# Token columns at other offsets in the rows of the operand tiles

## The chip, the cores and the metric

The kernel runs on one core of a Trainium2 chip. The metric is the device time of one execution in microseconds. The median over three runs of the kernel before is 2046.26 us (2046.22 to 2054.05).

## The reference

One layer of a hybrid decoder on 2048 prompt tokens and 64 sample tokens (8 sequences of 8), all in float32. It normalises x, makes one combined input projection, and runs three branches on its columns: windowed attention (A), a gated short convolution (B) and a chunked spatial MLP (C). Each branch is multiplied with a SiLU path and projected back to the model's width, weighted by a sigmoid gate, summed ("merged") and projected once more:

```python
xn = _rmsnorm(x, p["norm_w"])                       # (tokens, 1024)
h = jnp.einsum("btd,de->bte", xn, p["w_in"])        # all branch inputs and gates
a = jnp.einsum("bte,ed->btd", jax.nn.silu(z_a) * y_a, p["w_out_a"])
b = jnp.einsum("bte,ed->btd", jax.nn.silu(z_b) * y_b, p["w_out_b"])
c = jnp.einsum("bte,ed->btd", jax.nn.silu(z_c) * y_c, p["w_out_c"])
m = gates[:, :, 0] * a + gates[:, :, 1] * b + gates[:, :, 2] * c
return x + jnp.einsum("btd,de->bte", m, p["w_o"])
```

Keys, values, convolution rows and the sample's chunk rows are returned too. The change touches neither their values nor those of y.

## The kernel before, in words

The 2112 tokens are worked through in four super-blocks (the list `SBS`). The first three hold 512 prompt tokens each; the last holds 512 prompt tokens and the 64 sample tokens, and is cut into two chunks of 288 columns. Within a super-block the phases follow one another: keys and values (`kv_phase`), queries (`q_phase`), the z path of A with the attention units spread over it, convolution (`conv_phase`), MLP (`chunk_phase`), gates and merge (`gate_phase`), output projection (`out_phase`).

Every float32 operand of a large matmul is kept as two float32r tiles: a high part, cast on ScalarE (L169), and the low rest, subtracted on VectorE (L170). `gemm_t` multiplies such pairs. For each of 8 (or, for the branches, 4) slices of the contraction it issues three matmuls, at L178, L179 and L180: high weights by high data, high weights by low data, low weights by high data. A weight slice of 128 by 128 is the stationary operand, and 512 (in the last super-block 288) token columns are the moving one. Each matmul has its own weight load.

The data tiles lie in SBUF with the channel on the partition, and with one row of TMAX = 576 float32 columns (2304 bytes) for each slice of the contraction. There are four families:

- `xh`, `xl`: the normalised x, 8 rows each, allocated once;
- `mh`, `ml`: the merged branches, 8 rows each, allocated in `gate_phase`;
- `br0h` to `br2l`: the three branches' outputs, 4 rows each;
- the weights `wh`, `wl`, four buffers each, refilled in turn. They are the stationary operand of `gemm_t`. In `natural` and `wide`, which make keys, values, queries and the MLP's v with the tokens on the partition, the roles are exchanged: slices of 128 tokens of `xh` and `xl` are the stationary operand and the weights move.

In the built program each of these tiles begins at a multiple of 256 bytes. Rows are 2304 bytes (9 times 256), so that every row does too. In the first three super-blocks the 512 token columns start at column 0 of the row. In the last, the first chunk starts at column 0 and the second at column 288, 1152 bytes into the row, which is 128 bytes past a multiple of 256. `xr`, `mr` and `brr` are the functions that give `gemm_t` its moving slices; `xsplit` and `first_block` write `xh` and `xl`.

The order on TensorE and on the DMA queue is the order in the source. Small pieces of work (attention units, preparation of the next super-block) are queued with `later` and put between the matmuls by a count of matmul work (`tick`).

Of the kernel before, what the change touches and what calls it, by code (L numbers as in the profile page):

```python
# [11 lines left out]
F32R = mybir.dt.float32r  # L12
# [4 lines left out]
P = 128  # L17
# [9 lines left out]
TMAX = 576  # L27
# [7 lines left out]
AT_QUERIES, AT_SCORES, AT_PROBS, PROBS_EVERY, AT_VALUES = 0.25, 1.75, 3.5, 0.5, 5.25  # L35
AT_SPATIAL, SPATIAL_EVERY, SPATIAL_AFTER = 2.0, 0.3, 0.35
NEG = -1e30


SBS = [  # L40
# [8 lines left out]
def trunk_kernel(ctx: ExitStack, tc: tile.TileContext, A, O):  # L49
# [118 lines left out]
    def split(hi, lo, src):  # L168
        nc.scalar.copy(hi, src)  # L169
        nc.vector.tensor_tensor(lo, src, hi.bitcast(F32), ALU.subtract)  # L170
# [10 lines left out]
            if k % 2:  # L181
                tick((c1 - c0) / 512 * 0.25)

    xr = (lambda k, a, b: xh[:, k, a:b], lambda k, a, b: xl[:, k, a:b])

    def t_tiles(j, chunks):

# [41 lines left out]
    def xsplit(sb, st):  # L229
        t0, _, chunks, _ = SBS[sb]  # L230
        n = chunks[-1][1]

        def load(k):
            st[k] = st["x"][:, k % 4 * TMAX:k % 4 * TMAX + n]
            nc.sync.dma_start(st[k], A["xt"][k, :, t0 * P:t0 * P + n])

        def piece(k):
            if not k:
                for j in range(4):
                    load(j)  # L240
            x = st[k]
            nc.vector.scalar_tensor_tensor(x, x, nw[:, k:k + 1], st["r"], ALU.mult, ALU.mult)
            split(xh[:, k, :n], xl[:, k, :n], x)
            if k < 4:
                load(k + 4)

        return [lambda k=k: piece(k) for k in range(KT)]

    def first_block():

        xin = res.tile([P, 8 * TMAX], F32, tag="mh", name="xin")
        xnat = res.tile([P, 8 * TMAX], F32, tag="ml", name="xnat")
        r = small.tile([P, 8], F32, tag="xr", name="xr")
        rbuf = res.tile([P, 4 * TMAX], F32, tag="za", name="xrbuf")
        view = lambda t, i: t[:, i * D:(i + 1) * D].rearrange("p (k t) -> p k t", k=KT)

        def load(i, natural):
            if natural:
                nc.sync.dma_start(xnat[:, i * D:(i + 1) * D], A["xn"][i * P:(i + 1) * P])
            else:  # L260
                nc.sync.dma_start(view(xin, i), A["xt"][:, :, i * P:(i + 1) * P].rearrange("k p t -> p k t"))

        def piece(i):
            sq, x = xnat[:, i * D:(i + 1) * D], view(xin, i)
            nc.scalar.activation(sq, sq, AF.Square, accum_out=r[:, i:i + 1])
            rstd(r[:, i:i + 1], r[:, i:i + 1], 1, D)
            ps = ps_tp()
            nc.tensor.transpose(ps[:, 0:P], r[:, i:i + 1].broadcast_to([P, P]), ident)
            ts = slice(i * P, (i + 1) * P)
            rb = rbuf[:, ts]  # L270
            nc.scalar.copy(rb, ps[:, 0:P])
            for k in range(KT):
                nc.vector.scalar_tensor_tensor(x[:, k], x[:, k], nw[:, k:k + 1], rb, ALU.mult, ALU.mult)
                split(xh[:, k, ts], xl[:, k, ts], x[:, k])
            if i == 3:
                ahead.update(loads=RAWS, splits=AHEAD)

        return load, piece


    def natural(o, i, rows, units, n=256):

        ts = slice(i * P, i * P + rows)
        for k in range(KT):
            wh, wl = units[k // 4]
            ws = slice((k % 4) * n, (k % 4 + 1) * n)
            nc.tensor.matmul(o, xh[:, k, ts], wh[:, ws], start=k == 0, stop=False)  # L287
            nc.tensor.matmul(o, xh[:, k, ts], wl[:, ws], start=False, stop=False)  # L288
            nc.tensor.matmul(o, xl[:, k, ts], wh[:, ws], start=False, stop=k == KT - 1)  # L289
            if k % 4 == 3:  # L290
                tick(0.25)
        return o
# [10 lines left out]
    def wide(j0, outs):  # L303

        for u in range(4):
            wh, wl = take("wn", j0 + u)
            for i, (o, rows) in enumerate(outs):
                ts = slice(i * P, i * P + rows)
                for kk in range(2):
                    k = 2 * u + kk  # L310
                    ws = slice(kk * 512, (kk + 1) * 512)
                    nc.tensor.matmul(o, xh[:, k, ts], wh[:, ws], start=k == 0, stop=False)  # L312
                    nc.tensor.matmul(o, xh[:, k, ts], wl[:, ws], start=False, stop=False)  # L313
                    nc.tensor.matmul(o, xl[:, k, ts], wh[:, ws], start=False, stop=k == KT - 1)  # L314
                tick(0.25)
                if u == 3:
                    yield i, o, rows
# [201 lines left out]
    def sample_attention(samp, sbuf, za, br):  # L519
# [85 lines left out]
        later(4.0, lambda: probs(1))  # L605
        later(5.0, values)

    def conv_phase(sb, br):
        _, _, chunks, sample = SBS[sb]
        n = chunks[-1][1]  # L610
        for c in range(4):
            cs = tmp("cs", [P, n])
            for ps, c0, c1 in t_tiles(4 + 4 * c, chunks):
                nc.scalar.copy(cs[:, c0:c1], ps)
            cin = tmp("cin", [P, n + 2])
            nc.vector.tensor_copy(cin[:, 0:2], hist[:, c])
            for ps, c0, c1 in t_tiles(5 + 4 * c, chunks):
                nc.vector.tensor_tensor(cin[:, 2 + c0:2 + c1], ps, cs[:, c0:c1], ALU.mult)
            nc.vector.tensor_copy(hist[:, c], cin[:, 512:514])
            t1 = tmp("t1", [P, n])  # L620
            nc.vector.tensor_scalar_mul(t1[:, 0:512], cin[:, 0:512], cw[:, c, 0:1])
            for r in (1, 2):
                nc.vector.scalar_tensor_tensor(
                    t1[:, 0:512], cin[:, r:r + 512], cw[:, c, r:r + 1], t1[:, 0:512], ALU.mult, ALU.add
                )
            if sample:
                sc = small.tile([P, NS, TS + 2], F32, tag="scin", name="scin", bufs=1)
                nc.sync.dma_start(sc[:, :, 0:2], A["state"][:, c])
                nc.vector.tensor_copy(sc[:, :, 2:], cin[:, 514:578].rearrange("p (n t) -> p n t", n=NS))
                t1s = t1[:, 512:576].rearrange("p (n t) -> p n t", n=NS)  # L630
                nc.vector.tensor_scalar_mul(t1s, sc[:, :, 0:TS], cw[:, c, 0:1])
                for r in (1, 2):
                    nc.vector.scalar_tensor_tensor(t1s, sc[:, :, r:r + TS], cw[:, c, r:r + 1], t1s, ALU.mult, ALU.add)
                nc.sync.dma_start(O["sc"][:, c], sc[:, :, TS:])
                nc.sync.dma_start(O["pc"][:, c], hist[:, c])
            for ps, c0, c1 in t_tiles(6 + 4 * c, chunks):
                nc.vector.tensor_tensor(t1[:, c0:c1], ps, t1[:, c0:c1], ALU.mult)
            z = tmp("z", [P, n])
            for ps, c0, c1 in t_tiles(7 + 4 * c, chunks):
                nc.scalar.activation(z[:, c0:c1], ps, AF.Silu)  # L640
            nc.vector.tensor_tensor(t1, t1, z, ALU.mult)
            split(br[1][0][:, c, :n], br[1][1][:, c, :n], t1)

    def chunk_phase(sb, br, samp_args):
# [9 lines left out]
            for ps, c0, c1 in t_tiles(21 + 2 * c, chunks):  # L654
                nc.vector.tensor_tensor(suc[:, c, c0:c1], ps, suc[:, c, c0:c1], ALU.mult)
        flush()
        br2 = [res.tile([P, 4, TMAX], F32R, tag="br2" + x, name="br2" + x) for x in "hl"]
        br.append(br2)
        vbuf = res.tile([P, 4 * 1024], F32R, tag="mh", name="vbuf")
        def mixed(i, rows, t, gg):  # L660
# [55 lines left out]
    def gate_phase(sb, br):  # L716
        chunks = SBS[sb][2]
        n = chunks[-1][1]
        m = None
        for d in range(KT):  # L720
            acc = None
            for b in range(3):
# [6 lines left out]
                if d == 0 and b == 2:  # L729
                    flush()  # L730
                    m = [res.tile([P, KT, TMAX], F32R, tag="m" + x, name="m" + x) for x in "hl"]
                    if sb + 1 < len(SBS):
                        st, xpieces = xrstd(sb + 1)
                        for j, p in enumerate(xpieces):
                            later(2.0 + 4.0 * j, p)
                    if not sb:
                        later(4.0, lambda: keep("sk", "ck"))
                        later(12.0, lambda: keep("sv", "cvr"))
# [80 lines left out]

    for sb in range(len(SBS)):  # L820
        chunks, sample = SBS[sb][2:]
        samp = kv_phase(sb, None if sb else prepare)
        qn, abuf = q_phase(sb, samp)
        flush()
        if not sb:
            spatial_weights()
        za = res.tile([P, 4, TMAX], F32, tag="za", name="za")
        br = [[res.tile([P, 4, TMAX], F32R, tag=f"br{b}{x}", name=f"br{b}{x}") for x in "hl"] for b in range(2)]
        sbuf = attention(sb, qn, abuf, za, br, 0.0, UNIT_EVERY)
        for c in range(4):  # L830
            for ps, c0, c1 in t_tiles(c, chunks):
                nc.scalar.activation(za[:, c, c0:c1], ps, AF.Silu)
        conv_phase(sb, br)
        chunk_phase(sb, br, (samp, sbuf, za, br))
        m = gate_phase(sb, br)
        out_phase(sb, m)
# [124 lines left out]
```

## Time and profile before

| | |
|---|---|
| median of the runs | 2046.26 us |
| the profiled execution | 2048.72 us |
| its span, first to last instruction | 2047.0 us |
| mean granted TensorE clock | 0.995 |
| TensorE matmuls, busy share | 99% (10887 instructions) |
| weight loads | 86% |
| VectorE, ScalarE, GpSimd | 51%, 41%, 4% |

The profile was taken from one execution, so 2047.0 us is the time against which its rows add up; the execution's own time is 1.7 us longer. A matmul's duration in it runs from its start to a modelled end and overlaps the next matmul. The pace of a stream of matmuls is therefore read from the starts in the timeline, not from the durations.

### The profile page before, as it was taken

To read this page: it belongs to the slowest core of one execution; us is meant where nothing else is said; L and a number is where in the kernel's file an instruction comes from. 1 tells how busy PE (TensorE), PEld (TensorE's weight loads), DVE (VectorE), ACT (ScalarE), POOL (GpSimd) and SP (SyncE) were. 2 spreads that over 40 slices of the span, in tenths; PEclk is the share of its full clock that TensorE was granted. 3 is DMA by queue.
4 is the path that set the end of the run, shared out by engine and by line. 5 is a ranking of instruction groups with operands and counts; after the bars stand their busy time and mean duration, and the time that the engine had idled before them with its cause. 6 is when DMAs were issued, how large, how long until landed. Compare 5 with 4: busy or idle time off the path is not lost.

```text
span 2047.0 us, 27359 instructions
## 1 busy us (share of the span) xinstructions
PE 2016.7 (99%) x10887; PEld 1757.1 (86%) x10887; DVE 1050.9 (51%) x1818; ACT 845.8 (41%) x1462; POOL 83.5 (4%) x134
## 2 busy tenths in 40 slices
PE   6999999999999999999999999999999999999999
PEld 5788888888888888888888888888879999999999
DVE  5686263445588353335478535335537842533332
ACT  4675233332476333333267433333247641322320
POOL 2200000000200000000200000000110000000000
PEclk9999999999999999999999999999999998999999
DMA  6222233336222223336322223334522332222233
GB/s 206 82 83 83 84 101 123 114 119 210 84 82 83 88 78 126 111 93 201 119 83 81 84 82 109 118 108 136 173 83 59 64 114 57 65 85 86 78 104 108
DMA packets 85695, 212.25 MB, mean 104 GB/s; under 512 B 18224, under 2 KB 23344, under 8 KB 85552
## 3 DMA queue, kind: packets, MB, share of 16 engines
q1 hardware_dynamic: 85536, 209.53, 33.2%
q8 instruction: 85, 1.39, 0.3%
q10 hardware_dynamic: 32, 0.98, 0.1%
q14 instruction: 42, 0.34, 0.1%
HBM read 201.46 MB, written 10.00 MB: 103 GB/s over the span
## 4 chain that ended last, share of the span: by engine, by line
PE 93%; DVE 3%; ACT 2%; POOL 1%; issue 0%; DMA 0%; SPq 0%; ACTq 0%; DVEq 0%; POOLq 0%
PE ps_mm L179 26%; PE ps_mm L178 26%; PE ps_mm L180 26%; PE ps_tp L488 1%; PE wideS L313 1%; PE wideS L314 1%; PE wideS L312 1%; POOL qr L166 1%; PE ps_mm L312 1%; PE ps_mm L314 1%; PE ps_mm L313 1%; PE sp L464 1%; PE ps_mm L289 1%; PE ps_mm L287 1%; PE ps_mm L288 1%; PE pv L496 1%
## 5 line engine op out<-in xcount | busy, mean ns | idle before, releaser
L178 PE MATMUL ps_mm<-xh,wh 128*128 128x512 f32 (+1 forms) x2080 | 743.3, 357 | 5.0 <-DVE qn L409 4.5
L180 PE MATMUL ps_mm<-xh,wl 128*128 128x512 f32 (+1 forms) x2080 | 734.4, 353 | 0.0
L179 PE MATMUL ps_mm<-xl,wh 128*128 128x512 f32 (+1 forms) x2080 | 734.3, 353 | 0.0
L170 DVE TENSOR_TENSOR wl<-raw,wh 128x1024 fp32r<-128x1024 f32 x376 | 408.0, 1085 | 576.5 <-ACT wh L169 573.8
L169 ACT CAST wh<-raw 128x1024 fp32r<-128x1024 f32 x376 | 353.5, 941 | 772.1 <-PE ps_mm L179 535.4
L178 PEld LDWEIGHTS ps_mm<-xh,wh 128*128 128x128 f32 x2080 | 393.2, 189 | 51.9 <-issue 4.7
L180 PEld LDWEIGHTS ps_mm<-xh,wl 128*128 128x128 f32 x2080 | 392.6, 189 | 49.6
L179 PEld LDWEIGHTS ps_mm<-xl,wh 128*128 128x128 f32 x2080 | 393.4, 189 | 45.7
L179 PE MATMUL ps_mm<-ml,wh 128*128 128x512 f32 (+1 forms) x320 | 112.5, 351 | 0.3 <-DVE ml L170 0.3
L180 PE MATMUL ps_mm<-mh,wl 128*128 128x512 f32 (+1 forms) x320 | 112.4, 351 | 0.0
L178 PE MATMUL ps_mm<-mh,wh 128*128 128x512 f32 (+1 forms) x320 | 112.4, 351 | 0.0
L744 DVE TENSOR_TENSOR t<-ps_mm,t 128x512 f32<-128x512 f32 (+1 forms) x120 | 71.6, 597 | 73.7 <-PE ps_mm L180 73.7
L728 ACT ACTIVATE t<-ps_mm,c_bg 128x512 f32<-128x512 f32 (+1 forms) x120 | 73.0, 609 | 69.5 <-PE ps_mm L180 69.5
L450 ACT ACTIVATE rbuf<-ps_tp,c_qnw 64x256 fp32r<-64x256 f32 x128 | 60.0, 468 | 39.4 <-DVE rbuf L451 33.4
L179 PEld LDWEIGHTS ps_mm<-ml,wh 128*128 128x128 f32 x320 | 60.0, 188 | 8.0 <-DVE ml L170 0.6
L180 PEld LDWEIGHTS ps_mm<-mh,wl 128*128 128x128 f32 x320 | 60.1, 188 | 7.5
L178 PEld LDWEIGHTS ps_mm<-mh,wh 128*128 128x128 f32 x320 | 60.1, 188 | 7.4
L474 ACT ACTIVATE sbuf<-sbuf,nm 128x256 f32<-128x256 f32 (+1 forms) x128 | 62.8, 492 | 7.1 <-DVE nm L471 6.8
L767 DVE TENSOR_TENSOR xt<-ps_mm,xt 128x512 f32<-128x512 f32 (+1 forms) x40 | 23.9, 597 | 75.1 <-PE ps_mm L180 46.2
L179 PE MATMUL ps_mm<-br2l,wh 128*128 128x512 f32 (+1 forms) x160 | 56.5, 353 | 0.4 <-DVE br2l L170 0.2
L180 PE MATMUL ps_mm<-br2h,wl 128*128 128x512 f32 (+1 forms) x160 | 56.3, 352 | 0.0
L179 PE MATMUL ps_mm<-br1l,wh 128*128 128x512 f32 (+1 forms) x160 | 56.2, 352 | 0.0
(212 smaller groups left out, 2703.3 us busy)
## 6 DMA issues: line engine op xcount, KB each, us to landing
raw<-in_wt SPq DMA_DIRECT2D x208, 512.0 KB
raw<-in_wout SPq DMA_DIRECT2D x96, 256.0 KB
raw<-in_wn SPq DMA_DIRECT2D x40, 512.0 KB
raw<-in_wo SPq DMA_DIRECT2D x32, 512.0 KB
xbuf<-in_xn SPq DMA_DIRECT2D x12, 512.0 KB
xt<-in_xt SPq DMA_DIRECT2D x24, 256.0 KB
out_yt<-xt SPq DMA_DIRECT2D x24, 256.0 KB
xbuf<-in_xt SPq DMA_DIRECT2D x16, 256.0 KB
```

Source lines behind the costliest of these rows:

```text
L169: nc.scalar.copy(hi, src)
L170: nc.vector.tensor_tensor(lo, src, hi.bitcast(F32), ALU.subtract)
L178: nc.tensor.matmul(o, wh[:, ws], rh(k, c0, c1), start=k == 0, stop=False)
L179: nc.tensor.matmul(o, wh[:, ws], rl(k, c0, c1), start=False, stop=False)
L180: nc.tensor.matmul(o, wl[:, ws], rh(k, c0, c1), start=False, stop=k == kts - 1)
L312: nc.tensor.matmul(o, xh[:, k, ts], wh[:, ws], start=k == 0, stop=False)
L313: nc.tensor.matmul(o, xh[:, k, ts], wl[:, ws], start=False, stop=False)
L314: nc.tensor.matmul(o, xl[:, k, ts], wh[:, ws], start=False, stop=k == KT - 1)
L450: nc.scalar.activation(hh[half, :, e], src, AF.Copy, scale=qnw2[es])
L474: nc.scalar.activation(s[:, h, k0:], s[:, h, k0:], AF.Exp, bias=nm[:, h:h + 1], accum_out=den[:, h:h + 1])
L728: nc.scalar.activation(t[:, c0:c1], pg[:, : c1 - c0], AF.Sigmoid, bias=bg[:, 8 * b + d:8 * b + d + 1])
L744: nc.vector.tensor_tensor(t[:, c0:c1], pa[:, : c1 - c0], t[:, c0:c1], ALU.mult)
```

## The change

A table gives three offsets, in columns of 4 bytes, for each super-block: for the x tiles, the merged tiles and the branch tiles. The token columns of these tiles are written and read that many columns further right in their rows. The last super-block fills its 576 columns and keeps offset 0.

```diff
+SHIFT = [(4, 1, 20), (12, 6, 8), (2, 32, 14), (0, 0, 0)]
...
-    xr = (lambda k, a, b: xh[:, k, a:b], lambda k, a, b: xl[:, k, a:b])
+    off = [0]
+    xr = tuple(lambda k, a, b, t=t: t[:, k, off[0] + a:off[0] + b] for t in (xh, xl))
...
-            split(xh[:, k, :n], xl[:, k, :n], x)
+            o = SHIFT[sb][0]
+            split(xh[:, k, o:o + n], xl[:, k, o:o + n], x)
...
-                split(xh[:, k, ts], xl[:, k, ts], x[:, k])
+                os = slice(SHIFT[0][0] + i * P, SHIFT[0][0] + (i + 1) * P)
+                split(xh[:, k, os], xl[:, k, os], x[:, k])
...
-        ts = slice(i * P, i * P + rows)
+        ts = slice(off[0] + i * P, off[0] + i * P + rows)
...
+    def branch(sb, name):
+        t = res.tile([P, 4, TMAX], F32R, tag=name, name=name)
+        return t[:, :, SHIFT[sb][2]:SHIFT[sb][2] + SBS[sb][2][-1][1]]
...
-        br2 = [res.tile([P, 4, TMAX], F32R, tag="br2" + x, name="br2" + x) for x in "hl"]
+        br2 = [branch(sb, "br2" + x) for x in "hl"]
...
+                    m = [x[:, :, SHIFT[sb][1]:SHIFT[sb][1] + n] for x in m]
...
     for sb in range(len(SBS)):
         chunks, sample = SBS[sb][2:]
+        off[0] = SHIFT[sb][0]
...
-        br = [[res.tile([P, 4, TMAX], F32R, tag=f"br{b}{x}", name=f"br{b}{x}") for x in "hl"] for b in range(2)]
+        br = [[branch(sb, f"br{b}{x}") for x in "hl"] for b in range(2)]
```

In bytes, the token columns then begin at these places of a row:

| super-block | x | merged | branches |
|---|---|---|---|
| 0 | 16 | 4 | 80 |
| 1 | 48 | 24 | 32 |
| 2 | 8 | 128 | 56 |
| 3 | 0 | 0 | 0 |

The tiles themselves stay where they are, and so do the weights. The instructions of every engine, their order, their sizes and the semaphores that they wait for are the same as before, row for row; only start addresses within the three families differ.

More of the change, by code (lines that the diff above doesn't have):

```diff
@@ L307, in wide @@
             for i, (o, rows) in enumerate(outs):
-                ts = slice(i * P, i * P + rows)
+                ts = slice(off[0] + i * P, off[0] + i * P + rows)
                 for kk in range(2):
```

## The prediction

> **What bounds the kernel now.** I read the page first, then the chain of waits, then the four super-blocks as windows, and last the timeline of TensorE, since its durations overlap.
>
> The page's first part, and the shares of the chain of waits by engine:
>
> ```profile
> PE 2016.7 (99%) x10887; PEld 1757.1 (86%) x10887; DVE 1050.9 (51%) x1818; ACT 845.8 (41%) x1462; POOL 83.5 (4%) x134
> ...
> PE 93%; DVE 3%; ACT 2%; POOL 1%; issue 0%; DMA 0%; SPq 0%; ACTq 0%; DVEq 0%; POOLq 0%
> ```
>
> TensorE is never long without a matmul, and the chain lies on it for 93% of the span. VectorE and ScalarE have half their time free. So the time is the number of matmuls times their pace, and an edit counts if it changes that pace or makes TensorE wait.
>
> The windows of the four super-blocks (us, PE busy with its count, PEld, DVE, ACT, POOL, granted clock, DMA share, GB/s):
>
> ```profile
> 0.00:501.00 501.00, 482.60 (x2226) 400.79 (x2227) 271.09 (x488) 219.88 (x389) 25.79 (x44) 1.00 0.38 120
> 501.00:981.00 480.00, 478.51 (x2239) 398.64 (x2238) 256.05 (x420) 203.03 (x339) 18.40 (x28) 1.00 0.35 108
> 981.00:1462.00 481.00, 479.49 (x2238) 399.38 (x2237) 257.42 (x420) 204.95 (x342) 19.14 (x30) 1.00 0.35 109
> 1462.00:2047.00 585.00, 576.10 (x4189) 558.30 (x4187) 266.38 (x490) 217.93 (x392) 20.13 (x32) 0.99 0.28 82
> ```
>
> The granted clock is full in the first three, the ones that the change touches. Their idle time is 18 us in the first and 1.5 us in each of the next two.
>
> Now the pace itself. The timeline of TensorE in an output projection of super-block 1: two starts of the same line, 24 matmuls apart.
>
> ```profile
> 970.21 0.39 PE L178 MATMUL ps_mm<-mh,wh 128*128 128x512 f32 x1
> ...
> 975.65 0.39 PE L178 MATMUL ps_mm<-mh,wh 128*128 128x512 f32 x1
> ```
>
> 5.44 us for 24 matmuls is **226.7 ns** each. The same in the last super-block, where the second chunk (from 128 bytes past a multiple of 256) runs from 2033.71 to 2036.91, and then a first chunk (from a multiple of 256) to 2040.07, again 24 matmuls each:
>
> ```profile
> 2033.71 0.29 PE L178 MATMUL ps_mm<-mh,wh 128*128 128x288 f32 x1
> ...
> 2036.91 0.29 PE L178 MATMUL ps_mm<-mh,wh 128*128 128x288 f32 x1
> ...
> 2040.07 0.30 PE L178 MATMUL ps_mm<-mh,wh 128*128 128x288 f32 x1
> ```
>
> That is 133.3 ns for the second chunk and 131.7 ns for the first. Same weights, same width, same engine work around them: only the start of the moving operand differs, by 1152 bytes, and **the pace differs by 1.7 ns**. This is the one comparison in this trace of two placements, and it says that placement is not wholly without effect.
>
> From 512 and 288 columns a slope follows: (226.7 - 133.3) / 224 = 0.417 ns for a column. 512 columns are then 213.4 ns, and **13.3 ns** of every matmul are something else (11.7 ns in the first chunk). What it is, the rows show only in part. The stream after four transposes in super-block 0:
>
> ```profile
> 180.28 0.40 PE L179 MATMUL ps_mm<-xl,wh 128*128 128x512 f32 x1
> ...
> 182.13 0.39 PE L178 MATMUL ps_mm<-xh,wh 128*128 128x512 f32 x1
> ```
>
> Eight matmuls in 1.85 us: 231.3 ns each, 4.6 ns slower than the settled stream, with nothing but their history to tell them from it. The weight loads run beside the matmuls and begin with them:
>
> ```profile
> 2036.91 0.29 PE L178 MATMUL ps_mm<-mh,wh 128*128 128x288 f32 x1
> 2036.92 0.19 PEld L179 LDWEIGHTS ps_mm<-ml,wh 128*128 128x128 f32 x1
> ```
>
> So the fixed part depends on how the reading of the moving columns and the next weight load fall against each other in time, and a stream needs some ten matmuls to find its settled place. I read it as two streams that meet at SBUF; that is an interpretation, and the trace names no cause.
>
> **The change part by part.** It adds and removes no instruction, moves none, and changes no size and no wait. What is left are addresses.
>
> *Moving operands.* The matmuls of `gemm_t` in the first three super-blocks all start elsewhere in their rows. Their count is the 512-wide groups:
>
> ```profile
> L178 PE MATMUL ps_mm<-xh,wh 128*128 128x512 f32 x1248 | 493.2, 395 | 0.0
> ...
> L178 PE MATMUL ps_mm<-mh,wh 128*128 128x512 f32 x192 | 74.7, 389 | 0.0
> ...
> L178 PE MATMUL ps_mm<-br1h,wh 128*128 128x512 f32 x96 | 37.4, 390 | 0.0
> ```
>
> Each of these has two like it at L179 and L180, and there are three branches: 3 x (1248 + 192 + 3 x 96) = **5184** matmuls. At 226.7 ns they are 1175 us, so a nanosecond on each is 5.2 us of the whole.
>
> The price per matmul is in no row, since before no 512-wide operand starts off a multiple of 256. Its bounds: downwards the whole fixed part, -13.3 ns, which is -68.9 us; upwards the unsettled stream as a lasting state, +4.6 ns, which is +23.8 us. The nearest row is the pair of chunks, where a placement took 1.7 ns off. I take **-2.5 ns**: a fifth of the fixed part, nearer to that row than to the end, and more than it because eight of the nine new placements are off a multiple of 64 bytes, so that the two streams no longer begin in step. 5184 x 2.5 ns = **-13.0 us**. The sign is the weak point: the same pair of rows can be read as +1.7 ns for the chunk that starts off the multiple.
>
> By the page "TensorE: Matmul & The Clock Gate" of the Trainium skill (Back-to-back issue gap) a warm matmul of 512 columns takes N/2.4 + 2.5 ns, 215.8 ns. Here the trace does not agree: 226.7 ns. If the offsets brought all 5184 to that figure, the estimate by this page would be -56 us, inside the bound above.
>
> *Stationary operands.* In `wide` and `natural` the shifted x tiles are the stationary operand:
>
> ```profile
> L312 PE MATMUL wideS<-wh,xh 128*128 128x512 f32 x128 | 50.5, 394 | 0.0
> ...
> L287 PE MATMUL ps_mm<-wh,xh 128*128 128x256 f32 x128 | 38.9, 304 | 5.7 <-ACT xh L169 5.7
> ```
>
> With the groups into the other PSUM tiles, three quarters of 3 x 256 and of 3 x 128 are in the first three super-blocks, 864 matmuls. Between the same bounds they are worth -11.5 to +4.0 us. The weight load beside them has room (its 0.19 us against 0.227), so I take nothing.
>
> *Writes.* ScalarE and VectorE write the shifted tiles:
>
> ```profile
> L169 ACT CAST mh<-t 128x512 fp32r<-128x512 f32 x24 | 14.9, 621 | 34.2 <-DVE t L748 34.2
> ...
> L170 DVE TENSOR_TENSOR ml<-t,mh 128x512 fp32r<-128x512 f32 x24 | 16.6, 692 | 13.1 <-ACT mh L169 13.1
> ```
>
> If an unaligned write were a tenth slower, that is 0.06 us an instruction, behind engines that are busy half the time. TensorE waits for these tiles almost nowhere but in the first block:
>
> ```profile
> PE ps_mm L287 <- ACT xh L169: 5.7, 5, 4.3
> ...
> PE ps_mm L289 <- DVE xl L170: 0.9, 2, 0.7
> PE ps_mm L179 <- DVE ml L170: 0.3, 1, 0.3
> PE ps_mm L179 <- DVE br2l L170: 0.2, 1, 0.2
> ```
>
> 7.1 us in all; a tenth on it is 0.7 us. I take nothing, and +0.7 us as the upper end. No DMA reads or writes the shifted tiles, so the queues are as before.
>
> *Sum.* -13.0 us on the profiled span of 2047.0 us gives 2034.0 us. The median of the runs stands 0.7 us below that span; the same difference on the median gives 2046.26 - 13.0 = **2033 us**, 0.6% less. A measurement of this kernel can tell about 0.5% from no change.
>
> **Rivals.**
>
> *No effect.* The settled pace is 226.7 ns whatever the offset, because the fixed part is a hand-over inside TensorE that knows no address. For it: the 512-wide rows of x, merged and branch tiles all run at one pace although their rows and the weight buffers lie at many addresses, and the second chunk's 133.3 ns is just the slope plus the same 13.3 ns. Against it: the first chunk's 131.7 ns. It gives 2046 us, with the other terms 2040 to 2050.
> "TensorE: Matmul & The Clock Gate" of the Trainium skill (Step-by-step: what each phase is for) is on this side: it says that TensorE has two independent read ports into SBUF and that loading the next weights takes no bandwidth from the running matmul. If so, two starts could not clash, and the estimate is no change; the 1.7 ns between the chunks and the 4.6 ns of the unsettled stream are what this trace has against it.
>
> *Slower: the streams no longer settle.* With all starts at multiples of 256 bytes the three operands of a step are alike, and the pattern settles after some ten matmuls. With a start off such a multiple each row needs a further piece of memory at its end, and the phase found may be the unsettled one for good. Place: every `gemm_t` of the first three super-blocks. Price: 4.6 ns x 5184 = +23.8 us, 2070 us. It decides from a mean pace of 228.7 ns on (+2.0 ns x 5184 = 10.4 us, 0.5%). For it: the 231.3 ns stretch exists, and so does the second chunk's higher pace. Against it: the unsettled stream passes by itself each time.
>
> *Much faster.* The whole fixed part, or half of it, is a clash that the offsets remove: -6.7 ns to -13.3 ns, -35 to -69 us, 2012 to 1977 us. For it: 13.3 ns is much for a hand-over beside a weight load that has long ended. Against it: no placement in the trace comes near it.
>
> *The change does not do what it says.* Addresses that stay the same would give 2046 us. The slices are plain column offsets on both the writing and the reading side, so I give this 1 in 100, within "no effect".
>
> **How the numbers follow.** Forecast, a few nanoseconds less (2012 to 2041 us): 0.33. Much faster: 0.12. No effect: 0.29. Slower: 0.26. Of the forecast's 0.33 about 0.05 ends within 0.5% (above 2036 us). So faster by over 0.5%: 0.28 + 0.12 = 0.40; within 0.5%: 0.29 + 0.05 = 0.34; slower: 0.26. The range for 8 in 10 leaves about a tenth below, for a removal of more than 8 ns on each matmul (5184 x 8.3 ns = 43 us, 2003 us), and a tenth above for a price over the unsettled stream's: 2003 to 2070 us. As both signs hold much, the likeliest case's own range, 2012 to 2041 us, stands beside it.
>
> **What would show it.** In the changed profile the 24-matmul distances in an output projection of super-blocks 0, 1 and 2 would be about 5.38 us instead of 5.44; 5.44 in all three is the no-effect case, 5.55 the slower one, 5.28 or less much faster. The paces may differ among the three super-blocks and among x, merged and branch tiles, and show which offset does what. The last super-block must stay at 585 us and at 133.3 and 131.7 ns. VectorE's and ScalarE's means for the shifted writes, 692 and 621 ns, should stay; if they grow and TensorE's waits with them, the path was in the writes after all. If the clock in the first three windows falls below 1.00, the cause is none of these.

## The result

The changed kernel takes 2076.35 us (median), against 2047.92 us for the kernel before in the same comparison: a ratio of **1.0131**, 95% interval 1.0103 to 1.0159. It is slower by 1.3%; the forecast was 2033 us, 0.6% faster, and the range ended at 2070 us. Of the four executions of the changed kernel three lie between 2074.96 and 2076.80 us; the fourth took 5313.27 us at full clock, was not profiled, and stands outside the ratio. The profiled execution took 2076.8 us with a span of 2075.1 us, 28.1 us more than before.

The windows of the changed kernel, cut where its super-blocks begin (columns as before):

```profile
0.00:512.00 512.00, 493.56 (x2227) 401.64 (x2228) 271.41 (x488) 220.19 (x389) 25.58 (x44) 0.99 0.38 118
512.00:1002.00 490.00, 489.03 (x2239) 399.72 (x2238) 256.17 (x420) 202.88 (x340) 18.40 (x28) 1.00 0.34 106
1002.00:1492.00 490.00, 488.98 (x2241) 400.11 (x2240) 257.32 (x421) 204.40 (x343) 19.17 (x31) 1.00 0.34 107
1492.00:2075.00 583.00, 574.20 (x4185) 556.39 (x4184) 266.16 (x490) 217.53 (x392) 20.00 (x32) 0.99 0.28 82
```

The counts of matmuls per super-block are those of before to within four. Each of the first three windows is 9 to 11 us longer, and TensorE is busy for all of it: idle time is again 18 us in the first and 1 us in the next two. The last super-block, whose offsets are 0, kept its time. So the loss is pace, and it lies exactly where the offsets are. The granted clock of the first window reads 0.99 instead of 1.00, which the prediction had named as a sign against itself. It comes from the stretch of 10 to 100 us (0.96); the kernel with all offsets at 64 columns, below, has the same 0.96 there and takes the time of the kernel before, and from 100 us to the end of the third super-block the clock is 1.00. So it is not the cause.

The timeline of TensorE in the three output projections, first matmuls of two tiles, 144 matmuls apart:

```profile
472.50 0.40 PE L180 MATMUL ps_mm<-mh,wh 128*128 128x512 f32 x1
...
506.58 0.40 PE L180 MATMUL ps_mm<-mh,wh 128*128 128x512 f32 x1
...
962.70 0.40 PE L180 MATMUL ps_mm<-mh,wh 128*128 128x512 f32 x1
...
996.30 0.39 PE L180 MATMUL ps_mm<-mh,wh 128*128 128x512 f32 x1
...
1452.52 0.39 PE L180 MATMUL ps_mm<-mh,wh 128*128 128x512 f32 x1
...
1486.12 0.39 PE L180 MATMUL ps_mm<-mh,wh 128*128 128x512 f32 x1
```

34.08, 33.60 and 33.60 us: **236.7 ns** a matmul with the merged tile at column 1, **233.3 ns** at column 6, **233.3 ns** at column 32, where it was 226.7 ns in all three.

Where the rest went, from the groups of TensorE by shape: first two of before, then the same and the merged one of the changed kernel (its L181 and L182 are L179 and L180 of before).

```profile
L180 PE MATMUL ps_mm<-xh,wl 128*128 128x512 f32 x1248 | 487.3, 390 | 0.0
L179 PE MATMUL ps_mm<-xl,wh 128*128 128x512 f32 x1248 | 487.2, 390 | 0.0
```

```profile
L180 PE MATMUL ps_mm<-xh,wh 128*128 128x512 f32 x1248 | 499.6, 400 | 0.0
L181 PE MATMUL ps_mm<-xl,wh 128*128 128x512 f32 x1248 | 493.8, 396 | 0.0
L182 PE MATMUL ps_mm<-xh,wl 128*128 128x512 f32 x1248 | 493.3, 395 | 0.0
...
L181 PE MATMUL ps_mm<-ml,wh 128*128 128x512 f32 x192 | 76.1, 396 | 0.0
```

The x groups grew by 6.4, 6.6 and 6.0 us, 19.0 us together; the merged ones by 1.4 us each (74.7 before), 4.2 us. These are sums of modelled durations. Added up from each start to the next, the x matmuls took 19.2 us more, the merged ones 4.5 and the branches 3.8: 27.4 us for the 5184 matmuls, **5.3 ns** each. The wide phases have another 4.4 us, and the remaining matmuls took some 4 us less, which is no more than executions of one kernel differ by. The other engines did not change. The groups of ScalarE and VectorE that write the merged tiles:

```profile
L171 ACT CAST mh<-t 128x512 fp32r<-128x512 f32 x24 | 14.9, 622 | 34.5 <-DVE t L758 34.5
...
L172 DVE TENSOR_TENSOR ml<-t,mh 128x512 fp32r<-128x512 f32 x24 | 16.6, 692 | 13.2 <-ACT mh L171 13.1
```

And the waits of TensorE for the x tiles (us in total, times, longest):

```profile
PE ps_mm L292 <- ACT xh L171: 5.2, 6, 3.5
```

A shifted write takes 622 and 692 ns as before (621 and 692), and TensorE waits 5.2 us for them instead of 5.7.

### The profile page after: what moved, and what is told of

The parts are those of the page before. It is cut to its first block, busy times and chain, and to the rows that moved or that the text cites. A ratio compares the mean times of both kernels' runs of the same rounds, so it can differ in the third digit from the quotient of the medians.

```text
span 2075.1 us, 27359 instructions
## 1 busy us (share of the span) xinstructions
PE 2045.8 (99%) x10887; PEld 1757.8 (85%) x10887; DVE 1051.1 (51%) x1818; ACT 845.0 (41%) x1462; POOL 83.2 (4%) x134
## 4 chain that ended last, share of the span: by engine, by line
PE 92%; DVE 3%; POOL 2%; ACT 1%; issue 1%; DMA 0%; SPq 0%; ACTq 0%; DVEq 0%; POOLq 0%
PE ps_mm L181 26%; PE ps_mm L180 26%; PE ps_mm L182 26%; PE ps_tp L493 1%; PE wideS L318 1%; PE wideS L319 1%; PE wideS L317 1%; POOL qr L168 1%; PE sp L469 1%; PE ps_mm L317 1%; PE ps_mm L319 1%; PE ps_mm L318 1%; PE sp L468 1%; PE pv L500 1%; PE pv L501 1%
## 5 line engine op out<-in xcount | busy, mean ns | idle before, releaser
L180 PE MATMUL ps_mm<-xh,wh 128*128 128x512 f32 (+1 forms) x2080 | 748.8, 360 | 5.0 <-DVE qn L414 4.5
L181 PE MATMUL ps_mm<-xl,wh 128*128 128x512 f32 (+1 forms) x2080 | 740.2, 356 | 0.0
L182 PE MATMUL ps_mm<-xh,wl 128*128 128x512 f32 (+1 forms) x2080 | 739.7, 356 | 0.0
L180 PEld LDWEIGHTS ps_mm<-xh,wh 128*128 128x128 f32 x2080 | 393.3, 189 | 57.1 <-issue 4.7
L182 PEld LDWEIGHTS ps_mm<-xh,wl 128*128 128x128 f32 x2080 | 392.7, 189 | 55.2
L181 PEld LDWEIGHTS ps_mm<-xl,wh 128*128 128x128 f32 x2080 | 393.6, 189 | 50.4
L181 PE MATMUL ps_mm<-ml,wh 128*128 128x512 f32 (+1 forms) x320 | 113.9, 356 | 0.3 <-DVE ml L172 0.3
L182 PE MATMUL ps_mm<-mh,wl 128*128 128x512 f32 (+1 forms) x320 | 113.8, 356 | 0.0
L180 PE MATMUL ps_mm<-mh,wh 128*128 128x512 f32 (+1 forms) x320 | 113.8, 355 | 0.0
L181 PEld LDWEIGHTS ps_mm<-ml,wh 128*128 128x128 f32 x320 | 60.1, 188 | 9.5 <-DVE ml L172 0.6
L180 PEld LDWEIGHTS ps_mm<-mh,wh 128*128 128x128 f32 x320 | 60.1, 188 | 8.9
L182 PEld LDWEIGHTS ps_mm<-mh,wl 128*128 128x128 f32 x320 | 60.1, 188 | 8.9
L181 PE MATMUL ps_mm<-br2l,wh 128*128 128x512 f32 (+1 forms) x160 | 56.9, 356 | 0.2
L182 PE MATMUL ps_mm<-br2h,wl 128*128 128x512 f32 (+1 forms) x160 | 56.7, 355 | 0.0
L182 PE MATMUL ps_mm<-br0h,wl 128*128 128x512 f32 (+1 forms) x160 | 56.7, 354 | 0.0
```

The lines of the kernel that those rows point to most:

```text
L180: nc.tensor.matmul(o, wh[:, ws], rh(k, c0, c1), start=k == 0, stop=False)
L181: nc.tensor.matmul(o, wh[:, ws], rl(k, c0, c1), start=False, stop=False)
L182: nc.tensor.matmul(o, wl[:, ws], rh(k, c0, c1), start=False, stop=k == kts - 1)
```

## The experiments

The question is what "elsewhere" means to TensorE: the absolute start of the moving operand, its place against the weight load beside it, or any start but the first column. Unless something else is said, a pace is the distance of the first and last row shown over the 144 matmuls between them, in an output projection.

### Offsets of 256, 128 and 64 bytes

```diff
-SHIFT = [(4, 1, 20), (12, 6, 8), (2, 32, 14), (0, 0, 0)]
+SHIFT = [(64, 64, 64), (32, 32, 32), (16, 16, 16), (0, 0, 0)]
```

> All three families at column 64 (256 bytes) in super-block 0, 32 (128 bytes) in 1 and 16 (64 bytes) in 2. Theory A (the moving operand's absolute start counts: a read of 512 columns that begins off a multiple of 256 bytes touches one more piece): output projection 226.7 ns a matmul in super-block 0 and 233.3 ns, as the change has it at 128 bytes, in 1 and 2. Theory B (only the position of moving operand and weight load to each other counts, modulo 256 bytes): the same three numbers. Theory C (any other start than the row's first column costs): 231 to 237 ns in all three. Theory D (a piece is 64 bytes): 226.7 ns in all three, which the 233.3 ns at 128 bytes in the change already speaks against.

Timeline of TensorE, super-blocks 0, 1 and 2 in turn:

```profile
461.69 0.39 PE L180 MATMUL ps_mm<-mh,wh 128*128 128x512 f32 x1
...
494.33 0.39 PE L180 MATMUL ps_mm<-mh,wh 128*128 128x512 f32 x1
...
949.62 0.39 PE L180 MATMUL ps_mm<-mh,wh 128*128 128x512 f32 x1
...
983.08 0.40 PE L180 MATMUL ps_mm<-mh,wh 128*128 128x512 f32 x1
...
1434.19 0.39 PE L180 MATMUL ps_mm<-mh,wh 128*128 128x512 f32 x1
...
1467.15 0.39 PE L180 MATMUL ps_mm<-mh,wh 128*128 128x512 f32 x1
```

226.7 ns at 64 columns, 232.4 ns at 32, 228.9 ns at 16. Theories C and D fall: the shift as such is free at 256 bytes, and multiples of 64 bytes are not free. A and B both stand in outline; neither had 228.9 ns.

### Offsets of 4, 16 and 32 bytes

```diff
+SHIFT = [(1, 1, 1), (4, 4, 4), (8, 8, 8), (0, 0, 0)]
```

> All three families at column 1 (4 bytes) in super-block 0, 4 (16 bytes) in 1 and 8 (32 bytes) in 2. If every start off 256 bytes costs the same further piece: 233.3 ns in the output projection of all three. If the odd column costs more by itself, as the merged tile's 236.7 ns at 4 bytes in the change suggests: 236.7 ns in super-block 0, 233.3 ns or less in 1 and 2. If 16 or 32 bytes are a unit of reading: 226.7 ns in 1 or 2. Whole: about 2080 us.

```profile
478.50 0.40 PE L180 MATMUL ps_mm<-mh,wh 128*128 128x512 f32 x1
...
512.58 0.40 PE L180 MATMUL ps_mm<-mh,wh 128*128 128x512 f32 x1
...
966.61 0.40 PE L180 MATMUL ps_mm<-mh,wh 128*128 128x512 f32 x1
...
999.97 0.40 PE L180 MATMUL ps_mm<-mh,wh 128*128 128x512 f32 x1
```

236.7 ns at column 1, as in the change; 231.7 ns at 4; super-block 2, at 8, has 233.3 ns. The span is 2079.8 us. The odd column costs most of the three, and 16 or 32 bytes are no free unit.

### Everything 128 bytes further, weights included

An unused pad tile ahead of the large tiles is made smaller. No column is shifted.

```diff
-    consts.tile([P, 48], F32, name="pad")
+    consts.tile([P, 16], F32, name="pad")
```

> The kernel before, with its unused pad tile 128 bytes smaller, so that all large tiles, weights included, begin 128 bytes past a multiple of 256, and no column is shifted. Theory A (absolute start): every 512-wide matmul at 233.3 ns, the span about 35 us longer. Theory B (position to each other): 226.7 ns, the span as before, 2046 us. The second chunk of the last super-block then starts at a multiple of 256: A has 131.7 ns for it and 133.3 ns for the first, B 133.3 and 131.7 as before.

Super-block 0 in its output projection, and then three chunk starts of the last super-block, 24 matmuls apart: a first chunk to 2030.91, a second to 2034.11.

```profile
463.29 0.39 PE L178 MATMUL ps_mm<-mh,wh 128*128 128x512 f32 x1
...
495.93 0.39 PE L178 MATMUL ps_mm<-mh,wh 128*128 128x512 f32 x1
...
2027.75 0.29 PE L178 MATMUL ps_mm<-mh,wh 128*128 128x288 f32 x1
...
2030.91 0.29 PE L178 MATMUL ps_mm<-mh,wh 128*128 128x288 f32 x1
...
2034.11 0.29 PE L178 MATMUL ps_mm<-mh,wh 128*128 128x288 f32 x1
```

226.7 ns, and a span of 2044.2 us. Every moving operand starts 128 bytes off, where the change had 233.3 ns, and nothing is lost. The chunks keep their paces too, 131.7 and 133.3 ns, although now the second starts at a multiple of 256. **The absolute start (theory A) is refuted**: what counts is where the moving operand lies against something that moved along.

### Only the weights moved

The tile that lies just ahead of the weight buffers is made 8, and in another kernel 16, columns longer, so that the weights begin 32 or 64 bytes later while the three families stay. (The smaller buffers behind the weights move along; none of them is an operand of the matmuls whose paces are read here.) The *place* of a moving operand is from here on its start less that of the weights, in columns, modulo 64, which is 256 bytes.

```diff
-        st["r"] = res.tile([P, TMAX], F32, tag="acc", name="acc")[:, :n]
+        st["r"] = res.tile([P, TMAX + 8], F32, tag="acc", name="acc")[:, :n]
...
+SHIFT = [(0, 0, 0), (32, 32, 32), (48, 48, 48), (0, 0, 0)]
```

> All weight buffers begin 32 bytes later. Columns shifted by 0, 32 and 48 in super-blocks 0, 1 and 2, so that the moving operand stands at -8, +24 and +40 columns against the weights. Theory B: super-block 0 is slow although nothing of x, merged or branches is shifted in it: about 233 ns, as +8 was. The other two between 228 and 234 ns. The last super-block has -8 and +24 in its two chunks, where it had 0 and +32: no forecast of the sign, since 256-wide matmuls with shifted operands ran at 115.6 to 118.3 ns instead of 120.0; between 128 and 136 ns.

Super-block 0, in which no column is shifted:

```profile
474.46 0.40 PE L180 MATMUL ps_mm<-mh,wh 128*128 128x512 f32 x1
...
508.06 0.40 PE L180 MATMUL ps_mm<-mh,wh 128*128 128x512 f32 x1
```

233.3 ns: moving the weights alone costs what moving the data costs. The super-blocks at +24 and +40 columns have 233.3 and 234.3 ns. In the last one, at -8 and +24, the two chunks exchange their paces; a first chunk from 2065.43, a second to 2071.79:

```profile
2065.43 0.30 PE L180 MATMUL ps_mm<-mh,wh 128*128 128x288 f32 x1
...
2068.63 0.30 PE L180 MATMUL ps_mm<-mh,wh 128*128 128x288 f32 x1
...
2071.79 0.30 PE L180 MATMUL ps_mm<-mh,wh 128*128 128x288 f32 x1
```

133.3 ns in the first and 131.7 in the second. So a 288-wide stream at +24 is as fast as one at 0, where a 512-wide one loses 6.7 ns: which places cost something depends on the width.

The kernel with 16 columns, offsets 64, 13 and 16:

> All weight buffers begin 64 bytes later. Columns shifted by 64, 13 and 16: +48, -3 and 0 against the weights. Theory B: 226.7 ns in super-block 2, though both operands start off multiples of 256 bytes there; super-block 0 near the 228.9 ns that +16 had, if the pace is the same for -16; 231 to 237 ns in super-block 1. A theory in which a start off a multiple of 256 bytes costs by itself: 229 to 233 ns in super-block 2. The last super-block has -16 and +16 in its chunks: between 128 and 136 ns.

Super-blocks 1 and 2:

```profile
974.57 0.40 PE L180 MATMUL ps_mm<-mh,wh 128*128 128x512 f32 x1
...
1009.13 0.40 PE L180 MATMUL ps_mm<-mh,wh 128*128 128x512 f32 x1
...
1458.62 0.39 PE L180 MATMUL ps_mm<-mh,wh 128*128 128x512 f32 x1
...
1491.26 0.39 PE L180 MATMUL ps_mm<-mh,wh 128*128 128x512 f32 x1
```

Super-block 2 has operand and weights both 64 bytes off and runs at 226.7 ns: theory B is confirmed from both sides. Super-block 1, three columns before the weights, has 240.0 ns, the slowest found. Super-block 0, at +48, which is -16 modulo 64, has 233.3 ns and not the 228.9 of +16, so the sign matters. The two chunks of the last super-block, at -16 and +16, have 133.3 and 132.2 ns.

### One family undone

```diff
+SHIFT = [(0, 1, 20), (0, 6, 8), (0, 32, 14), (0, 0, 0)]
```

> The change with the x tiles back at column 0, merged and branch tiles shifted as in the change. If each matmul pays for the place of its own operands: 226.7 ns again wherever x is read, 236.7, 233.3 and 233.3 ns in the output projections, some 231 to 233 ns in the branch matmuls. 192 x (10.0 + 6.7 + 6.7) ns + 288 x (4.7 + 6.0 + 4.8) ns = 9.0 us over the kernel before: a span of about 2055 us, and 19 of the 28 us belong to x. If the loss came from writes or from elsewhere: not so divided.

```profile
core 0: 2053.2 us, clock 0.997
```

The kernel before, run beside it on the same chip, has a span of 2042.9 us at the same clock. So 10.3 us of the loss are left, where 9.0 were expected; from start to start the merged and branch matmuls have 8.3 of them. The other two thirds of the change's 28.1 us belong to x, as the group rows say, and the wide phases, where x is the stationary operand, are back at 226.7 ns from 233.3, 233.3 and 230.7 (the median over groups of six, start to start).

### Matched weights at fine offsets

The weights of the branch projections fill half of their buffers, so they can be put as far to the right as the branch tiles.

```diff
+            d = SHIFT[i * len(SBS) // len(units)][2] if n == 512 else 0
-            split(wh[:, :n], wl[:, :n], loaded[i][:, :n])
+            split(wh[:, d:d + n], wl[:, d:d + n], loaded[i][:, :n])
```

First with the change's offsets:

> The change, with the weights of the branch projections (512 columns in buffers of 1024) put as many columns to the right as the branch tiles: 20, 8 and 14. Theory B (the position of moving operand and weight load to each other): the branch matmuls go back to 226.7 ns but for a few after each gate tile, from 231.4, 232.7 and 231.4 ns; the span falls by about 4 us from the change's. If both ends must lie on a line of their own: no better than in the change, or worse, up to 236.7 ns.

This expectation failed. The branch matmuls ran at about 231 to 234 ns, hardly other than in the change, and the span is 2076.9 us. A possible reason is the shifted x matmuls around them, so the next kernel keeps x and merged tiles at column 0:

> x and merged tiles at column 0, the branch tiles at 20, 8 and 14 as in the change, and the weights of the branch projections the same number of columns to the right. The run before this one with matched branch weights had the x tiles shifted too, and its branch matmuls stayed at 230 to 234 ns. If that came from the shifted x stream around them (12 branch matmuls are too few to settle): 226.7 ns here in all three. If a common shift of 80, 32 or 56 bytes is not like one of 64 or 128 (start addresses within a smaller unit count by themselves): above 228 ns in one or more of the three.

and the last one takes 4, 16 and 24 columns for both:

> x and merged tiles at column 0, the branch tiles and the weights of the branch projections both at column 4 (16 bytes) in super-block 0, 16 (64 bytes) in 1, 24 (96 bytes) in 2. In the earlier run with both at 8 columns the branch matmuls came back to 226 and 227 ns after eight matmuls; at 20 and 14 they did not within their twelve. If a common shift must be a multiple of 32 bytes: super-blocks 1 and 2 settle to 226 and 227 ns within the twelve, 0 stays at 230 to 234 ns. If 64 bytes: only 1 settles. If any common shift does and the earlier failures were too short a stream: no such order.

A branch projection has only 12 matmuls between two gate tiles at column 0. Their distances in ns, read from the starts in the two traces, one projection of each offset:

```
 4 columns, 16 bytes   233 228 231 229 232 228 231 228 233 228 231 230
 8 columns, 32 bytes   231 223 231 237 228 232 231 226 227 227 226 235
14 columns, 56 bytes   234 235 233 231 236 233 231 236 233 231 237 236
16 columns, 64 bytes   228 230 232 237 224 230 236 228 233 231 227 226
20 columns, 80 bytes   230 234 230 232 232 230 231 231 231 231 232 232
24 columns, 96 bytes   236 233 235 225 231 236 227 233 230 228 226 227
```

At 8, 16 and 24 columns the stream reaches 226 to 227 ns before its end, at 4, 14 and 20 it does not within twelve. Taking the shift of x away was not enough: over all projections the mean is 231.4 and 233.8 ns at 20 and 14 columns. With a common shift by 32, 64 or 96 bytes the stream can reach its full pace, but it spends seven to ten distances on the way there: the means are 229.5, 230.1 and 231.4 ns at 8, 16 and 24 columns, where the kernel before has 226.8. The kernel with 4, 16 and 24 columns has a span of 2051.7 us, 4.2 us more than the kernel before beside it, so in these short streams matching the weights does not win the loss back. At 4 and 14 columns the distances repeat in turns of two and three from early on, which looks more like a lasting cycle than like a stream on its way. Whether it would last is not shown: no long stream could be given such a shift, because the other weights fill their buffers.

The whole kernel 32 bytes off, by the pad tile:

> The kernel before, with its unused pad tile 32 bytes smaller: all large tiles, weights included, begin 32 bytes before a multiple of 256, and no column is shifted. If only the place of operand and weight load to each other counts, down to 32 bytes: 226.7 ns everywhere and the span of the kernel before, within 4 us. If each must also lie on a multiple of 64 bytes: 231 to 234 ns and a span some 25 to 35 us longer.

```profile
462.27 0.39 PE L178 MATMUL ps_mm<-mh,wh 128*128 128x512 f32 x1
...
494.91 0.39 PE L178 MATMUL ps_mm<-mh,wh 128*128 128x512 f32 x1
```

226.7 ns, span 2045.8 us: 32 bytes in common are free in long streams too.

### Only the high or only the low tiles

The offsets of the high and of the low tiles are taken apart: low at 8 columns in super-block 0, high at 8 in 1, low at 32 in 2.

```diff
+SHIFT = [(0, 8), (8, 0), (0, 32), (0, 0)]
...
-                    m = [x[:, :, SHIFT[sb][1]:SHIFT[sb][1] + n] for x in m]
+                    m = [x[:, :, c:c + n] for x, c in zip(m, SHIFT[sb])]
```

> Only the low tiles (every third matmul's moving operand) at column 8 in super-block 0, only the high ones (two of three) at 8 in 1, only the low ones at 32 in 2. If each pair of a running matmul and the load beside it pays by itself: 226.7 + 6.7/3 = 228.9 ns in 0 and 2, 231.1 ns in 1. If one operand out of step keeps the whole stream from settling: 231 to 234 ns in all three.

```profile
473.32 0.40 PE L181 MATMUL ps_mm<-mh,wh 128*128 128x512 f32 x1
...
506.92 0.40 PE L181 MATMUL ps_mm<-mh,wh 128*128 128x512 f32 x1
...
960.52 0.39 PE L181 MATMUL ps_mm<-mh,wh 128*128 128x512 f32 x1
...
993.80 0.39 PE L181 MATMUL ps_mm<-mh,wh 128*128 128x512 f32 x1
```

233.3 ns with one operand in three out of place, as much as with all three; 231.1 ns with two in three, and 231.1 ns in super-block 2. The 231.1 ns of super-block 1 would also fit a toll on each shifted operand; the other two, where 228.9 ns was expected by it, do not. Nor do the single distances of super-block 0: they repeat 233, 236 and 231 ns, so all three matmuls are slow, and not only one in three. One operand out of place slows the whole stream. That fits a settled state that is lost, not a toll for each matmul.

### A shorter weight load

The output projection uses 64 weight columns in super-block 1 and 32 in 2, in the kernel before. It leaves the other output rows there without their projection:

```diff
-        o = ps[:, : c1 - c0]
+        o = ps[:mc, : c1 - c0]
...
-            ws = slice(k * P, (k + 1) * P)
+            ws = slice(k * P, k * P + mc)
```

> The kernel before, with the output projection using 64 of the 128 weight columns in super-block 1 and 32 in 2, and so computing half and a quarter of its output rows there (the rest keeps the residual x alone); super-blocks 0 and 3 as before. If the fixed 13.3 ns of a matmul come from the weight load's reads getting in the way of the moving operand's: about 6.7 ns and 3.3 ns are left, 220 ns in super-block 1 and 217 in 2. If they are a hand-over that knows nothing of the load's size: 226.7 ns in all.

```profile
944.69 0.40 PE L178 MATMUL ps_mm<-mh,wh 128*64 128x512 f32 x1
...
977.81 0.40 PE L178 MATMUL ps_mm<-mh,wh 128*64 128x512 f32 x1
...
1424.98 0.39 PE L178 MATMUL ps_mm<-mh,wh 128*32 128x512 f32 x1
...
1458.34 0.39 PE L178 MATMUL ps_mm<-mh,wh 128*32 128x512 f32 x1
```

230.0 and 231.7 ns: a smaller load, which also gives fewer output rows, is slower. Both theories fall, the hand-over that knows nothing of the load's size and the load that gets in the way by its length. With 96 columns, and with the merged tile at column 8 for the short loads:

> The output projection uses 96 weight columns in super-block 0, 64 in 1 and 32 in 2 (and computes only so many of each 128 output rows there), with the merged tiles at column 8 in 1 and 2 and nothing else shifted. With the merged tiles at column 0, 64 and 32 weight columns gave 230.0 and 231.7 ns. If the pace falls by 3.3 ns for each 64 further weight columns: 228.3 ns in super-block 0. If the place matters through the load's own reading, less of it leaves less to disturb, and all settle near one pace: 231 to 234 ns in 1 and 2, the shift adding less than the 6.7 ns that it adds at 128 columns. If the shift adds by itself: 236.7 and 238.3 ns.

```profile
463.86 0.39 PE L180 MATMUL ps_mm<-mh,wh 128*96 128x512 f32 x1
...
496.98 0.39 PE L180 MATMUL ps_mm<-mh,wh 128*96 128x512 f32 x1
...
944.20 0.39 PE L180 MATMUL ps_mm<-mh,wh 128*64 128x512 f32 x1
...
977.44 0.39 PE L180 MATMUL ps_mm<-mh,wh 128*64 128x512 f32 x1
```

230.0 ns at 96 columns, 230.8 ns at 64 with the shift (230.0 without), and 233.3 ns at 32 with the shift (231.7 without). Where the load is short the shift adds 0.8 and 1.7 ns, not 6.7. So 226.7 ns is a state that a 512-wide stream reaches with full loads in step with it; take away either, and it runs at 228.9 ns or more in these runs.

### The same mechanism at a harmless offset

```diff
+SHIFT = [(64, 64, 64), (64, 64, 64), (64, 64, 64), (0, 0, 0)]
```

> All three families at column 64 in super-blocks 0 to 2: the whole mechanism of the change, at an offset that keeps operands and weights at the same place modulo 256 bytes. If the loss is that place alone: 226.7 ns everywhere, a ratio to the kernel before within 0.3% of 1. If shifted writes or a start off the row's first column cost anything: longer, up to the change's 1.3%.

The ratio to the kernel before is 0.9999, interval 0.9989 to 1.0009. The slices, the shifted writes and starts that are not the row's first column cost nothing. The loss of the change is the choice of its numbers.

All paces of a 512-wide output projection with full loads, by the place of the moving operand against the weights, in columns modulo 64:

| columns | 0 | 1 | 4 | 6 | 8 | 16 | 24 | 32 | 40 | 48 | 56 | 61 |
|---|---|---|---|---|---|---|---|---|---|---|---|---|
| ns | 226.7 | 236.7 | 231.7 | 233.3 | 233.3 | 228.9 | 233.3 | 232.4 to 233.3 | 234.3 | 233.3 | 233.3 | 240.0 |

None of the eleven other places is as fast as 0, where the kernel before has its 512-wide operands.

## Why the prediction was wrong

**The bound** was read rightly. The time is the number of matmuls times their pace; no wait, write, queue or clock took part. The mean granted clock was 0.995 in both executions.

**The step that failed is the price per moving operand**, -2.5 ns, and in it the sign: the changed kernel shows +5.3 ns on average. I had two rows for it: 131.7 and 133.3 ns in the two chunks, and 231.3 ns after the transposes. I read the chunks as "a placement took 1.7 ns off", and argued that a start off 64 bytes would keep the two streams from beginning in step, and that this would help. The runs show the contrary for 512 columns: in step, at place 0, is the fast state. The first chunk is the one at place 0 and the second the one at 32, in whatever absolute place (shown by moving everything by 128 bytes). Read so, the pair of rows said +1.7 ns for leaving place 0. The prediction named this reading as its weak point and then took the other. But that reading too would have had the sign right by luck: when the weights alone moved, the 288-wide chunk at +24 was as fast as the one at 0. A pair of 288-wide rows could give neither size nor sign for 512 columns.

**The rival "the streams no longer settle"** is what happened. Its place is confirmed, every large matmul of the first three super-blocks; its cause nearly: a 512-wide stream at place 0 passes through 231 ns to 226.7 within ten matmuls, and elsewhere it stays at 229 to 240 ns over a whole output projection. Its price was set too low. 4.6 ns was taken as the upper bound because it was the slowest stretch in the trace, but a passing state is no bound on lasting ones: the merged tiles pay 10.0, 6.7 and 6.7 ns. The range ended at that bound, 2070 us, and so missed 2076 us. Its own reason, a further piece of memory at the end of each row, is refuted: rows that begin 128 bytes off run at full pace if the weights do too.

**"No effect"** rested on a hand-over that knows no address; a spread from 226.7 to 240.0 ns refutes it. "TensorE: Matmul & The Clock Gate" of the Trainium skill (Step-by-step: what each phase is for) says that the load has its own read port and takes no bandwidth from the running matmul. The step from there to no change does not hold for this stream: whatever the ports are, the pace depends on where the two operands lie against each other. Whether the load takes bandwidth, no run shows. "Much faster" had the fixed 13.3 ns as a clash that offsets remove; no place removed any of it. Nor are the 13.3 ns a firm size: their slope sets the 512-wide stream at place 0 against the 288-wide one at 32, and with the first chunk, at 0, the same sum leaves 9.6 ns.

**The stationary operands** were costed at nothing, with bounds of -11.5 to +4.0 us. The wide phases went to 233.3, 233.3 and 230.7 ns, 576 matmuls by 6.7, 6.7 and 4.0 ns, 3.3 us if all were settled. The cover that I named, a weight load of 0.19 us beside a matmul of 0.227, is no cover, since the load's length is not what is paid. The keys and values, 256 wide, went the other way, from 120.0 to 117.9 and 115.6 ns in super-blocks 1 and 2; with 96 matmuls in each that is 0.6 us.

**The writes** were right at nothing.

**What stays open** is what the fixed part of a matmul is, why the settled state of a 512-wide stream needs the same place modulo 256 bytes, and why a 288-wide one does not. That the moving reads and the loads' reads share something with a period of 256 bytes, and lock, fits the relative place, the settling, and the loss by one operand in three. That a shorter load is slower, and that a 288-wide stream is as fast at +24 as at 0, do not follow from it. This is a guess: no run looks inside.

## What to carry to other kernels

When a stream of 512-wide float32r matmuls, each with its own weight load, bounds a kernel, let the columns of the moving operand and of the weights start at the same place modulo 256 bytes (64 float32 columns), and check the pace by start-to-start distances: here every other place tried cost 1 to 6%. If one of them must be shifted, shift by 256 bytes, or shift both alike; 32, 64 and 128 bytes for both cost nothing in long streams. At other widths measure anew: at 288 columns +24 was as good as 0, and at 256 a shift gained. And when a trace holds two paces that differ by placement, ask first which of the two the kernel has now: if it has the settled one everywhere, as here in the first three super-blocks, a change of addresses has little to gain and much to lose. And before a loss is read from two spans, set each against the kernel before of its own round: in the rounds of these experiments that span lay between 2042.9 and 2049.6 us, at clocks of 0.997 and 0.993.

## What the runs showed of the hardware that was not expected

- The pace of float32r matmuls of 512 columns depends on the relative start of moving and stationary operand: 226.7 ns at equal places modulo 256 bytes, 228.9 ns at 64 bytes, 236.7 ns at 4 bytes and 240.0 ns at -12 bytes.
- One moving operand in three out of place by 8 columns slows the stream as much as all three, 233.3 ns.
- Fewer weight columns, and output rows with them, make it slower: 226.7 ns with 128, 230.0 with 96 or 64, 231.7 with 32.
- At 288 columns other places are fast: 131.7 ns at 0 and at +24, 132.2 at +16, 133.3 at +32, -8 and -16.
- At 256 columns a shifted stationary operand is faster, 115.6 ns at 2 columns against 120.0.
